# Triangular inverse of the RWKV-7 chunk scan: 32x32 diagonal blocks, off-diagonal block by two products

## The chip, the cores and the metric

One core of a Trainium2 chip runs the whole program. The metric is device time in microseconds (us) of one execution, the median of several runs. Engines: PE (TensorE matmul; PEld is its weight load), DVE (VectorE), ACT (ScalarE), POOL (GpSimd), SP (its queue issues most DMAs).

## The reference, cut to what matters

A first block (attention and a Mamba scan), then a second block of two layers on 512 tokens plus 256 context tokens. One half of layer 0 is an RWKV-7 mixer: 8 heads of 64 channels, run over the tokens in both directions.

```python
def rwkv7_scan(r, w, k, v, kk, b, s0):
    def step(s, inp):
        r_t, w_t, k_t, v_t, kk_t, b_t = inp
        sa = jnp.einsum('bhvk,bhk->bhv', s, kk_t)
        s = s * w_t[:, :, None, :] - sa[..., None] * b_t[:, :, None, :] + v_t[..., None] * k_t[:, :, None, :]
        return s, jnp.einsum('bhvk,bhk->bhv', s, r_t)
```

The kernel does not step token by token. It takes chunks of 64 tokens; inside a chunk the terms `sa` depend on each other through a triangular 64x64 matrix A per head, so the kernel needs the inverse of (I + A) for each head, direction and chunk.

## The kernel before, in words

The program is one long stream of weight units (512 KB of fp32 each) that SP loads into three buffers, ACT rounds (`whi`, L292), DVE takes the rest of (`wlo`, L293), and PE multiplies in three products (L301 to L303, L384 to L386). The scan of layer 0 runs inside that stream: `mix0_scan` (L1647) walks 12 steps, 4 on the context and 8 on the tokens, and between the pieces of a step it emits pieces of other work: the token projections and `rwkv_prep` first, then the context's output projection and FFN. The order on each engine is then set by a scheduler of the framework, which orders instructions by its own cost estimates before the program is built; on the chip each engine works its list in order.

A step treats one chunk per direction (d), 4 pairs of heads (b), and the two heads of a pair in the two halves of the partitions (e): 16 triangles of 64x64, held as a tile of 128 partitions x 512 columns (d, b, 64). Three generators make a step:

- `scores(i)` (L1504): loads AR, KB and v, multiplies them (L1513), masks (L1516, `Sc`), copies the triangle part into A (L1521, POOL for e = 0 and ACT for e = 1), then writes AR over the copied part of Sc (L1523).
- `inverse(i)` (L1543): level 0 on DVE (L1554, L1555, and L1557, a transpose into Tm), then five levels l = 1 to 5, each of which doubles the size of the inverted blocks: POOL masks the level's part out of A (`Al`, L1550); 16 matmuls Tm, Al (L1563); ACT copies the result out of PSUM into W (L1565); 16 matmuls with X and W (L1573); DVE subtracts (L1576) and transposes (L1577), or on the last level subtracts into X6 (L1581).
- `serial(i)` (L1584): F (L1603), U = X6 times f (L1609), the new state (L1616 to L1622), the output (L1629, L1632).

While step i is in `serial(i)` and then `scores(i+2)`, `inverse(i+1)` runs beside it (`tail`, L1676). These matmuls are fp32, and each appears as two rows of PE and two of PEld: 16 matmuls make 32 rows. They use a part of the array: `tile_position` gives its first row and column, so that the two heads of a pair sit in different quarters of the array.

```python
for d, b in DB:
    for e, h in enumerate(H):
        mm(ps[h, d, b], Al[h, d, b], Tm[h, d, b], start=True, stop=True, tile_position=(64 * e, 64 * e))
```

For comparison the text also uses L1030 (`ada_units`): fp32 matmuls of 128 rows into 32 columns with 256 moving columns, on four column strips of the array in turn, and L1041, fp32 matmuls with 128x128 weights and 32 moving columns.

## Time and profile before

| | |
|---|---|
| median of 3 runs | 3386.49 us (3383.27 to 3392.45) |
| the profiled execution | 3376.74 us |
| its span, first to last instruction | 3375.0 us |
| PE busy | 3163.2 us, 94% |
| DVE busy | 2023.6 us, 60% |
| ACT busy | 1378.6 us, 41% |
| POOL busy | 238.0 us, 7% |
| the scan | about 1390 to 2160 us of the span |

A row of a group of instructions reads: line, engine, operation, tile written <- tiles read, shape, count | busy us, mean ns of one | idle us of the engine just before them and what ended it. A row of a stretch gives start:end, its length, the busy us of PE, PEld, DVE, ACT and POOL with the number of instructions that ran in it, the granted clock of PE (1.00 is full), and the DMA share and rate. A matmul's own duration contains its way through the array; matmuls that follow each other overlap, so the distance between starts is what a matmul costs.

### The profile page before, as it was taken

What the parts mean: (1) busy time and instruction counts of PE and PEld (TensorE: products, weight loads), DVE (VectorE), ACT (ScalarE), POOL (GpSimd) and SP (SyncE); (2) the same over time, 40 slices, a digit from 0 to 9 for tenths busy, and PEclk for the clock granted to TensorE, in tenths of its full rate; (3) what the DMA queues carried; (4) which work ended last, traced back from release to release, by engine and by line L of the source; (5) the groups of instructions that cost most, each with busy time, mean ns of one, the idle gap of its engine ahead of it and who ended that gap; (6) DMA issues with size and microseconds to landing.
All of it is one profiled execution on the core that took longest, in us unless ns stands there. A gap on an engine that the chain in (4) does not pass through costs nothing.

```text
span 3375.0 us, 51306 instructions
## 1 busy us (share of the span) xinstructions
PE 3163.2 (94%) x20798; PEld 2539.0 (75%) x20798; DVE 2023.6 (60%) x3274; ACT 1378.6 (41%) x2301; POOL 238.0 (7%) x276
## 2 busy tenths in 40 slices
PE   8999999998899999888898999989999989899998
PEld 7777777776777788666677888768788767778886
DVE  3344576775556533557665666667475754776756
ACT  3344334332354432434344444456432444543323
POOL 0000000000100000121121122000000210000001
PEclk9999999999999999899899999999999999999999
DMA  6222344435434432444545554633322425232333
GB/s 205 81 70 70 120 156 137 134 123 190 163 114 131 131 111 94 134 125 118 159 162 173 163 170 148 203 136 99 106 94 94 137 91 184 72 113 89 99 99 108
DMA packets 216493, 430.85 MB, mean 128 GB/s; under 512 B 75114, under 2 KB 114218, under 8 KB 216000
## 3 DMA queue, kind: packets, MB, share of 16 engines
q1 hardware_dynamic: 192896, 367.83, 34.5%
q10 hardware_dynamic: 20912, 51.64, 4.1%
q0 software_dynamic: 2448, 8.09, 0.8%
q8 instruction: 164, 2.69, 0.3%
q14 instruction: 73, 0.60, 0.1%
HBM read 380.70 MB, written 46.79 MB: 127 GB/s over the span
## 4 chain that ended last, share of the span: by engine, by line
PE 76%; DVE 10%; DMA 6%; ACT 4%; issue 3%; POOL 1%; SPq 0%; ACTq 0%; POOLq 0%; DVEq 0%
PE psa L301 11%; PE psa L303 11%; PE psa L302 11%; PE psa L384 6%; PE psa L385 6%; PE psa L386 6%; PE pso L301 3%; PE pso L302 3%; PE pso L303 3%; DVE wlo L293 3%; PE psa L1563 1%; ACT whi L292 1%; PE psa L1573 1%; PE pso L1030 1%; PE pso L384 1%
## 5 line engine op out<-in xcount | busy, mean ns | idle before, releaser
L293 DVE TENSOR_TENSOR wlo<-wraw,whi 128x1024 fp32r<-128x1024 f32 x480 | 597.2, 1245 | 483.6 <-ACT whi L292 482.6
L292 ACT CAST whi<-wraw 128x1024 fp32r<-128x1024 f32 x482 | 503.7, 1046 | 740.1 <-PE psa L386 258.8
L301 PE MATMUL psa<-xh,wlo 128*128 128x512 f32 (+1 forms) x1760 | 693.4, 396 | 15.6 <-DVE wlo L293 12.1
L303 PE MATMUL psa<-xh,whi 128*128 128x512 f32 (+1 forms) x1760 | 685.0, 390 | 0.0
L302 PE MATMUL psa<-xl,whi 128*128 128x512 f32 (+1 forms) x1760 | 684.0, 390 | 0.0
L301 PEld LDWEIGHTS psa<-xh,wlo 128*128 128x128 f32 x1760 | 335.7, 192 | 95.0 <-DVE wlo L293 15.5
L303 PEld LDWEIGHTS psa<-xh,whi 128*128 128x128 f32 x1760 | 336.0, 191 | 72.5 <-issue 5.1
L302 PEld LDWEIGHTS psa<-xl,whi 128*128 128x128 f32 x1760 | 336.6, 192 | 70.6 <-issue 3.9
L1151 DVE SCALAR_TENSOR_TENSOR fc<-psa,f_cv,fc 128x441 f32<-128x441 f32 (+2 forms) x352 | 243.5, 693 | 41.4 <-ACT fc L1140 34.6
L301 PE MATMUL pso<-xh,wlo 128*128 128x256 f32 (+1 forms) x720 | 231.2, 321 | 0.0
L302 PE MATMUL pso<-xl,whi 128*128 128x256 f32 (+1 forms) x720 | 221.5, 308 | 1.0 <-DVE xl L347 1.0
L303 PE MATMUL pso<-xh,whi 128*128 128x256 f32 (+1 forms) x720 | 220.6, 306 | 0.0
L385 PE MATMUL psa<-wlo,ah 128*128 128x512 f32 x528 | 211.1, 400 | 2.8 <-DVE wlo L293 2.5
L384 PE MATMUL psa<-whi,al 128*128 128x512 f32 x528 | 209.2, 399 | 3.4 <-ACT whi L292 3.4
L386 PE MATMUL psa<-whi,ah 128*128 128x512 f32 x528 | 210.0, 398 | 0.0
L301 PEld LDWEIGHTS pso<-xh,wlo 128*128 128x128 f32 x720 | 136.4, 189 | 11.9 <-issue 1.7
L302 PEld LDWEIGHTS pso<-xl,whi 128*128 128x128 f32 x720 | 136.4, 189 | 9.8 <-issue 1.7
L303 PEld LDWEIGHTS pso<-xh,whi 128*128 128x128 f32 x720 | 136.2, 189 | 7.5 <-issue 0.4
L385 PEld LDWEIGHTS psa<-wlo,ah 128*128 128x128 f32 x528 | 99.2, 188 | 29.9 <-DVE wlo L293 6.3
L384 PEld LDWEIGHTS psa<-whi,al 128*128 128x128 f32 x528 | 99.0, 188 | 29.5 <-ACT whi L292 4.7
L384 PE MATMUL psa<-whi,xl 128*128 128x512 f32 x288 | 116.9, 408 | 4.4 <-DVE h L941 2.7
L385 PE MATMUL psa<-wlo,xh 128*128 128x512 f32 x288 | 116.8, 406 | 0.0
(559 smaller groups left out, 5119.1 us busy)
## 6 DMA issues: line engine op xcount, KB each, us to landing
wraw<-in_f_up_dram SPq DMA_DIRECT2D x132, 512.0 KB
wraw<-in_ada_w_dram SPq DMA_DIRECT2D x96, 512.0 KB
wraw<-in_f_dn_dram SPq DMA_DIRECT2D x66, 512.0 KB
wraw<-in_w_fi_dram SPq DMA_DIRECT2D x44, 512.0 KB
wraw<-in_ab_f_dram SPq DMA_DIRECT2D x38, 512.0 KB
wraw<-in_w_qk_dram SPq DMA_DIRECT2D x24, 512.0 KB
wraw<-in_w_xbc_dram SPq DMA_DIRECT2D x24, 512.0 KB
wraw<-in_c_f_dram SPq DMA_DIRECT2D x24, 512.0 KB
```

The costliest lines, as they stand in the source:

```text
L292: nc.scalar.copy(hi, raw)
L293: (eng or nc.vector).tensor_tensor(lo, raw, hi.bitcast(F32), op=ALU.subtract)
L301: mm(ps, wl, xh, start=start, stop=False)
L302: mm(ps, wh, xl, start=False, stop=False)
L303: mm(ps, wh, xh, start=False, stop=stop)
L384: mm(ps, sl, wh[:, c], start=first and k == 0, stop=False)
L385: mm(ps, sh, wl[:, c], start=False, stop=False)
L386: mm(ps, sh, wh[:, c], start=False, stop=last and k == kbn - 1)
L1030: nc.tensor.matmul(ps[o:o + 32], self.cs[:, 4 * h + j, 22 - 2 * i:54 - 2 * i], raw[:, j * 256:(j + 1) * 256], start=h == 0, stop=h == 1, t ...
L1151: V_.scalar_tensor_tensor(o, pv[:, r0 + dr:r1 + dr, c0 + dc:c1 + dc], cw(i), o, op0=ALU.mult, op1=ALU.add)
L1563: mm(ps[h, d, b], Al[h, d, b], Tm[h, d, b], start=True, stop=True, tile_position=(64 * e, 64 * e))
L1573: mm(ps[h, d, b], lt[h, d, b], rt[h, d, b], start=True, stop=True, tile_position=(64 * e, 64 * e))
```

## The change

The 64x64 triangle is cut into two 32x32 diagonal blocks and one 32x32 off-diagonal block. `A` holds the diagonal blocks of all four 32-partition strips in 256 columns, `Ao` the off-diagonal block in 128 columns (four copies of 32 partitions each on POOL and on ACT in place of one copy of 64 each). `inverse` runs levels 0 to 4 on the diagonal blocks, in tiles of 256 columns, with 32 matmuls of 32x32 on the four diagonal 32x32 tiles of the array in the place of 16 of 64x64. The last level becomes two products of 16 matmuls of 32x32 (`Ao` with `Tm`, then `Wo` with `X`). X6 is now one tile, set to zero once; the diagonal blocks are copied into it and the second product is written into it negated. The mask table shrinks from 1600 to 1120 columns.

```diff
-    for b in (1, 2, 4, 8, 16, 32):
-        lev.append(f2(((s // b) % 2 == 0) & (t // b == s // b + 1)))
-        lev.append(f2(((s // b) % 2 == 1) & (t // b == s // b - 1)))
-    lev.append(f2(s == t))
+    s, t = p % 32, np.arange(32)[None, :]
+    for b in (1, 2, 4, 8, 16):
+        lev.append(((s // b) % 2 == 0) & (t // b == s // b + 1))
+        lev.append(((s // b) % 2 == 1) & (t // b == s // b - 1))
+    lev.append(s == t)
...
+        Q = [[slice(64 * e + 32 * r, 64 * e + 32 * r + 32) for r in range(2)] for e in range(2)]
+        C = [slice(0, 32), slice(32, 64)]
+        X6 = pool.tile([P, 2, 4, 64], F32, name="X6", bufs=1)
+        G_.memset(X6, 0.0)
...
-            A = BA[i] = first.tile([P, 2, 4, 64], F32, name="A", bufs=1)
+            A = first.tile([P, 2, 4, 32], F32, name="A", bufs=1)
+            Ao = first.tile([P, 4, 32], F32, name="Ao", bufs=1)
+            BA[i] = A, Ao
             for e in range(2):
-                (G_.tensor_copy, S_.copy)[e](A[H[e]], Sc[H[e], :, e, :, 0])
+                for r in range(2):
+                    (G_.tensor_copy, S_.copy)[e](A[Q[e][r]], Sc[Q[e][r], :, e, :, 0, C[r]])
+                    (G_.tensor_copy, S_.copy)[e](Ao[Q[e][r]], Sc[Q[e][r], r, e, :, 0, C[1 - r]])
...
+            def prod(ps, lt, rt):
+                for d, b in DB:
+                    for q in range(4):
+                        h = slice(32 * q, 32 * q + 32)
+                        mm(ps[h, d, b], lt[h, d, b], rt[h, d, b], start=True, stop=True, tile_position=(32 * q, 32 * q))
...
-            for l in range(1, 6):
-                ps = v8(self.ptile())
-                for d, b in DB:
-                    for e, h in enumerate(H):
-                        mm(ps[h, d, b], Al[h, d, b], Tm[h, d, b], start=True, stop=True, tile_position=(64 * e, 64 * e))
-                W = new("W", 1)
+            for l in range(1, 5):
+                ps = w4(self.ptile())
+                prod(ps, Al, Tm)
+                W = part4("W", 1)
                 S_.copy(W, ps)
-                if l < 5:
+                if l < 4:
                     Al = part(l + 1)
                 yield
-                ps = v8(self.ptile())
-                for d, b in DB:
-                    for e, h in enumerate(H):
-                        lt, rt = (X, W) if l < 5 else (W, X)
-                        mm(ps[h, d, b], lt[h, d, b], rt[h, d, b], start=True, stop=True, tile_position=(64 * e, 64 * e))
-                if l < 5:
-                    Tn, Xn = new("Tm"), new("X")
-                    V_.tensor_tensor(Tn, Tm, ps, op=ALU.subtract)
-                    V_.transpose(fl(Xn), fl(Tn))
-                    Tm, X = Tn, Xn
-                else:
-                    XI[i] = new("X6", 1)
-                    V_.tensor_tensor(XI[i], X, ps, op=ALU.subtract)
-                yield
+                ps = w4(self.ptile())
+                prod(ps, X, W)
+                Tn, Xn = part4("Tm"), part4("X")
+                V_.tensor_tensor(Tn, Tm, ps, op=ALU.subtract)
+                V_.transpose(fl(Xn), fl(Tn))
+                Tm, X = Tn, Xn
+                yield
+            ps = self.ptile()[:, :128].rearrange("p (b v) -> p b v", b=4)
+            for b in range(4):
+                for e in range(2):
+                    for d in range(2):
+                        k, o = Q[e][d], Q[e][1 - d]
+                        mm(ps[o, b], Ao[k, b], Tm[k, d, b], start=True, stop=True, tile_position=(k.start, o.start))
+            W = pool.tile([P, 4, 32], F32, name="Wo", bufs=1)
+            S_.copy(W, ps)
+            for e in range(2):
+                for r in range(2):
+                    (G_.tensor_copy, S_.copy)[e](X6[Q[e][r], :, :, C[r]], X[Q[e][r]])
+            yield
+            ps = self.ptile()[:, :128].rearrange("p (b v) -> p b v", b=4)
+            for b in range(4):
+                for e in range(2):
+                    for d in range(2):
+                        k, o = Q[e][d], Q[e][1 - d]
+                        mm(ps[k, b], W[o, b], X[o, d, b], start=True, stop=True, tile_position=(o.start, k.start))
+            for e in range(2):
+                for d in range(2):
+                    dst, src = X6[Q[e][d], d, :, C[1 - d]], ps[Q[e][d]]
+                    if e:
+                        S_.activation(dst, src, AF.Copy, scale=-1.0)
+                    else:
+                        V_.tensor_scalar(dst, src, -1.0, None, op0=ALU.mult)
+            XI[i] = X6
+            yield
```

How the lists of the engines change is shown at three places. The first is PE in the last step but one, where U (X6 times f) is followed by the first products of the next inverse. Before:

```order
L386 MATMUL pso<-whi,ah 128x512
L1609 MATMUL psb<-f,X_18116 64x64 x16
L1563 MATMUL psa<-Tm,Al 64x64 x16
L301 MATMUL pso<-xh,wlo 128x256
L302 MATMUL pso<-xl,whi 128x256
```

And now (the line numbers are those of the changed file: L303 to L305 are the old L301 to L303, L1571 is the matmul in `prod`):

```order
L388 MATMUL pso<-whi,ah 128x512
L1648 MATMUL psb<-f,X_10640 64x64 x16
L1571 MATMUL psa<-Tm,Al 32x32 x32
L303 MATMUL pso<-xh,wlo 128x256
L304 MATMUL pso<-xl,whi 128x256
```

The burst stands at the same place between the same neighbours; 16 matmuls of 64x64 have become 32 of 32x32.

The second place is PE in the middle of the scan, at the end of an inverse. Before, the last burst of the last level:

```order
L303 MATMUL pso<-xh,whi 128x256
L1030 MATMUL pso<-wraw,cs 32x256 x8
L1539 MATMUL psb<-masks,KB_16369 128x128 x4
L1573 MATMUL psa<-X,W 64x64 x16
L301 MATMUL pso<-xh,wlo 128x256
```

Now, with L1612 the second product of the off-diagonal block:

```order
L305 MATMUL pso<-xh,whi 128x256
L1032 MATMUL pso<-wraw,cs 32x256 x8
L1550 MATMUL psb<-masks,KB_17538 128x128 x4
L1612 MATMUL psa<-X,Wo 32x32 x16
L303 MATMUL pso<-xh,wlo 128x256
```

Here 16 matmuls stay 16, of a quarter of the size, again at the same place.

The third place is ACT at the end of the same inverse. Before (L1521 and L1523 belong to the scores of the step after next, L292 to the weight units, L1140 and L1156 to the context's FFN):

```order
L1523 COPY Sc<-AR_16361 64x4x64
L1523 COPY Sc<-AR_16367 64x4x64
L1521 COPY A<-Sc 64x512
L1565 COPY W<-psa 128x512
L292 CAST whi<-wraw 128x1024
L1533 COPY vs<-psb 64x2x2x64 x2
L1140 ACTIVATE fc<-pso,f_cb,f_cv 128x256
L1540 COPY Ns<-psb 128x4x2x64
```

Now:

```order
L1531 COPY A<-Sc 32x256 x2
L1583 COPY W<-psa 128x256
L294 CAST whi<-wraw 128x1024
L1544 COPY vs<-psb 64x2x2x64 x2
L1605 COPY X_10640<-X 32x8x32 x2
L1142 ACTIVATE fc<-pso,f_cb,f_cv 128x256
L1551 COPY Ns<-psb 128x4x2x64
L1532 COPY Ao<-Sc 32x128
L1534 COPY Sc<-AR_17530 64x4x64
L1534 COPY Sc<-AR_17536 64x4x64
L1532 COPY Ao<-Sc 32x128
L1158 ACTIVATE fc<-fc 128x256
L1602 COPY Wo<-psa 128x128
```

The two copies of AR into Sc have moved from ahead of the A copy to the end of the inverse. They stand between the two copies of Ao, and Ao has one buffer, which the first off-diagonal product (L1600) of the running inverse still reads.

## Rows read from the trace of the kernel before

**Rows 1.** The page: PE's busy row, and the chain of waits by engine.
```profile
PE 3163.2 (94%) x20798; PEld 2539.0 (75%) x20798; DVE 2023.6 (60%) x3274; ACT 1378.6 (41%) x2301; POOL 238.0 (7%) x276
PE 76%; DVE 10%; DMA 6%; ACT 4%; issue 3%; POOL 1%; SPq 0%; ACTq 0%; POOLq 0%; DVEq 0%
```

**Rows 2.** Stretches of the scan: length, busy PE, PEld, DVE, ACT, POOL, clock.
```profile
1390.00:1700.00 310.00, 258.59 (x2702) 191.61 (x2700) 203.52 (x289) 138.03 (x255) 63.52 (x68) 0.87 0.45 132
1700.00:1850.00 150.00, 134.77 (x1911) 110.70 (x1908) 94.70 (x155) 61.98 (x117) 29.80 (x32) 0.95 0.51 168
1850.00:2160.00 310.00, 302.04 (x4149) 265.36 (x4149) 200.77 (x301) 146.65 (x230) 51.27 (x51) 1.00 0.50 159
```

**Rows 3.** Groups by line, 1390 to 2160 us: bursts of the inverse, and L1513.
```profile
L1563 PE MATMUL psa<-Tm,Al 64*64 64x64 f32 x1920 | 76.0, 230 | 16.7 <-DVE Tm L1576 11.8 <-POOL vs L1502 2.3 <-POOL Al L1550 1.3
L1573 PE MATMUL psa<-W,X 64*64 64x64 f32 x1536 | 57.7, 223 | 0.2 <-ACT W L1565 0.2
L1513 PE MATMUL psa<-AR,KB 64*128 64x128 f32 x384 | 32.5, 304 | 10.5 <-DMA AR<-za 5.4 <-DMA KB<-zk 5.1
```

**Rows 4.** Timeline of PE, three places: start us, us, line, rows in the burst.
```profile
1433.67 1.07 PE L1030 MATMUL pso<-wraw,cs 128*32 128x256 f32 x16
...
1447.10 1.15 PE L1563 MATMUL psa<-Tm,Al 64*64 64x64 f32 x32
...
1896.40 1.16 PE L1513 MATMUL psa<-AR,KB 64*128 64x128 f32 x16
1897.49 1.15 PE L1573 MATMUL psa<-W,X 64*64 64x64 f32 x32
```

**Rows 5.** Two short stretches at a burst's start: L1030, then L1563.
```profile
1433.66:1433.70 0.04, 0.03 (x4) 0.03 (x5) 1.00 0.00 0
...
1447.09:1447.14 0.05, 0.04 (x2) 0.04 (x2) 1.00 0.00 0
```

**Rows 6.** Stretches of 0.03 and 0.02 us at the start of one L1041 group.
```profile
660.68:660.71 0.03, 0.01 (x1) 0.01 (x1) 1.00 0.00 0
660.71:660.73 0.02, 0.02 (x2) 0.02 (x1) 1.00 0.50 205
```

**Rows 7.** Bursts of L1563 by stretch of the scan: busy us and count.
```profile
1390.00:1700.00 310.00, 26.65 (x640) 23.67 (x640) 0.87 0.45 132
1700.00:1850.00 150.00, 19.70 (x448) 16.94 (x448) 0.95 0.51 168
1850.00:2160.00 310.00, 29.69 (x832) 26.64 (x832) 1.00 0.50 159
```

**Rows 8.** Waits of PE from 1390 to 1850 us: us in total, times, longest.
```profile
PE pso L1415 <- DVE kds L1413: 11.2, 4, 4.1
PE psa L1563 <- DVE Tm L1576: 9.6, 5, 3.8
PE psa L1513 <- DMA AR<-za: 5.4, 2, 4.2
```

**Rows 9.** Waits of PE from 1850 to 2160 us.
```profile
PE psa L1563 <- POOL vs L1502: 2.3, 1, 2.3
PE psa L1563 <- DVE Tm L1576: 2.2, 4, 0.9
```

**Rows 10.** Groups by line, 1390 to 2160 us: the other engines.
```profile
L1565 ACT COPY W<-psa 128x512 f32<-128x512 f32 x60 | 35.1, 585 | 61.1 <-PE psa L1563 57.2 <-issue 2.9 <-ACT yo L1638 0.9
L1577 DVE STREAM_TRANSPOSE X<-Tm 128x512 f32<-128x512 f32 x48 | 33.9, 706 | 0.8
L1576 DVE TENSOR_TENSOR Tm<-Tm,psa 128x512 f32<-128x512 f32 x48 | 32.6, 680 | 18.3 <-PE psa L1573 18.3
L1550 POOL TENSOR_TENSOR Al<-A,masks 128x512 f32<-128x512 f32 x60 | 85.9, 1433 | 410.4 <-PE psa L1563 394.2 <-DVE xn L332 15.7
L1604 DVE COPY f<-psb 128x256 f32<-128x256 f32 x12 | 5.0, 418 | 6.0 <-PE psb L1603 5.9
L1604 ACT COPY f<-psb 128x256 f32<-128x256 f32 x12 | 4.5, 373 | 2.9 <-PE psb L1603 2.9
```

More of the change, by code (lines that the diff above doesn't have):

```diff
@@ L1543, in inverse @@
         def inverse(i):
-            A = BA.pop(i)
-            lev = lambda l: self.mlev[:, l].unsqueeze(2).to_broadcast([P, 2, 4, 64])
+            A, Ao = BA.pop(i)
+            lev = lambda l: self.mlev[:, l].unsqueeze(2).to_broadcast([P, 2, 4, 32])
+            part4 = lambda n, k=2: pool.tile([P, 2, 4, 32], F32, name=n, bufs=k)
+            w4 = lambda ps: ps[:, :256].rearrange("p (d b v) -> p d b v", d=2, b=4)
             def part(l):
-                r = new("Al")
+                r = part4("Al")
@@ L1550, in part @@
                 G_.tensor_tensor(r, A, lev(l), op=ALU.mult)
                 return r
+            def prod(ps, lt, rt):
[3 more added lines that the diff above has]
+                        mm(ps[h, d, b], lt[h, d, b], rt[h, d, b], start=True, stop=True, tile_position=(32 * q, 32 * q))
             Al = part(1)
-            X = new("X")
+            X = part4("X")
             V_.tensor_tensor(X, A, lev(0), op=ALU.mult)
-            V_.tensor_tensor(q8(X), self.id2.unsqueeze(1).to_broadcast([P, 8, 64]), q8(X), op=ALU.subtract)
@@ L1556, in inverse @@
-            Tm = new("Tm")
+            V_.tensor_tensor(q8(X), self.id2.unsqueeze(1).to_broadcast([P, 8, 32]), q8(X), op=ALU.subtract)
+            Tm = part4("Tm")
             V_.transpose(fl(Tm), fl(X))
             yield
-            for l in range(1, 6):
-                ps = v8(self.ptile())
-                for d, b in DB:
-                    for e, h in enumerate(H):
-                        mm(ps[h, d, b], Al[h, d, b], Tm[h, d, b], start=True, stop=True, tile_position=(64 * e, 64 * e))
-                W = new("W", 1)
+            for l in range(1, 5):
+                ps = w4(self.ptile())
+                prod(ps, Al, Tm)
+                W = part4("W", 1)
@@ L1608, in serial @@
                 for e, h in enumerate(H):
-                    mm(U[h, d, b], X6[h, d, b], f[h, d, b], start=True, stop=True, tile_position=(64 * e, 64 * e))
+                    mm(U[h, d, b], X6_[h, d, b], f[h, d, b], start=True, stop=True, tile_position=(64 * e, 64 * e))
             S_.activation(vu[H[0], :, 0], U[H[0]], AF.Copy, scale=-1.0)
```

10 lines of the change are left out of this document (5 added, 5 removed).

## The prediction

> **What bounds the kernel now.** I read the page first: PE is busy 94% of the span and holds 76% of the chain of waits [rows 1]. The change touches the scan only, so the next view is the scan in three stretches [rows 2]. They differ. From 1390 to 1700 us, where the context's and the tokens' inputs are still being prepared, PE is busy 258.6 of 310 us and its clock is 0.87 of full: there PE waits for others. From 1700 to 1850 us it is busy 134.8 of 150 us. From 1850 to 2160 us it is busy 302 of 310 us at full clock, with DVE at 201, ACT at 147 and POOL at 51 us: there PE alone sets the pace. The waits of PE say the same. Up to 1850 us the largest are for DVE's preparation of the inputs (11.2 us in four waits), for the subtraction of the inverse (9.6 us in five) and for a load (5.4 us) [rows 8]; after 1850 us the two largest are 2.3 and 2.2 us [rows 9]. The inverse's share: of the 1920 rows of L1563 in all, 640 lie in the first stretch, 448 in the second and 832 in the third [rows 7], so of the 12 inverses 4, 2.8 and 5.2. The scheduler's lists place every burst of the changed kernel between the same neighbours, so what a burst loses or gains PE meets at the same spot.
>
> **What a burst costs.** An inverse is ten bursts of 32 rows, each 1.15 us from first start to last end [rows 4]; a row alone lasts 0.22 to 0.23 us [rows 3]. That leaves 0.93 us from first to last start. Two rows start together, one per quarter of the array in use (two within 0.05 us [rows 5]), so the burst is 16 pairs, 0.93 / 15 = 0.062 us apart. The burst of L1513 has 16 rows with weights of 128 columns and 128 moving columns, also two by two; its rows last 0.30 us in the mean [rows 3], as little as 0.27 us by the same share as above, and the whole 1.16 us [rows 4], so 8 pairs are (1.16 - 0.27) / 7 = 0.127 us apart. Double the columns, double the distance: 0.065 us for 64 columns. Half of 64 columns should then take 0.062 - 0.032 = 0.030 us.
>
> **How many rows run side by side.** The new products use four separate tiles of the array in turn. The trace has no 32x32 tile. The nearest row is L1030, four column strips in turn: four of its rows start within 0.04 us [rows 5], and its 16 rows of 256 moving columns, 0.385 us each, are over in 1.07 us [rows 4], which only fits four at a time. Issuing is therefore fast enough for four rows in 0.04 us at a burst's start. Whether it holds over 64 rows is not shown: the fastest whole burst has 0.93 us for 32 rows, 0.029 us a row [rows 4]. These are the bounds for the price of a row: 0.030 / 4 = 0.0075 us (four side by side) and 0.029 us (no faster than seen over a whole burst). I take the lower end, since L1030 shows four tiles at once and the distance between rows has followed the columns so far; L1041 has two rows with 32 moving columns that both start within 0.05 us [rows 6], so a row so short need not hold the array for the 0.062 us of a 64-column pair.
>
> **The sum on PE.** A burst of 32 matmuls is 64 rows, 16 groups of four: 15 x 0.030 + 0.04 for the spread of four starts + 0.22 for the last row = 0.71, with a slightly longer first gap 0.73 us. A burst of 16 (the two off-diagonal products) is 8 groups: 7 x 0.030 + 0.04 + 0.22 = 0.47 us. One inverse: before 10 x 1.15 = 11.5 us, now 8 x 0.73 + 2 x 0.47 = 6.8 us, a gain of 4.7 us. The number of bursts stays ten, so what lies at a burst's edge is paid as often as before. Where the clock is at half a row saves twice as much; I leave that out.
>
> **What of it reaches the end.** Third stretch: 5.2 x 4.7 = 24.4 us, PE is the bound, I keep 95% (23). Second: 2.8 x 4.7 = 13.2 us, a tenth of the time PE waits; I keep 80% (10.5). First: 18.8 us, a sixth of the time PE waits, mostly on DVE's preparation, which does not get shorter with PE's burst; I keep half (9.4). Together 43 us.
>
> **The other engines.** DVE's work per inverse halves in columns: a subtraction of 512 columns takes 0.68 and a transpose 0.71 us; the row nearest to the new subtraction is the copy of 256 columns out of PSUM with 0.42 us [rows 10]. Four levels save about 4 x (0.27 + 0.33) = 2.4 us, level 0 and the last level about 1.2 us more. DVE is at 65% in the third stretch and waited for little, so I count nothing; if DVE were the bound, as in parts of the first stretch, it would add up to 3.6 us an inverse. POOL's mask of a level falls from 1.43 us towards half, one level goes, and six small copies come in place of one, none with more columns than a half mask; POOL is busy 51 of 310 us. The memset of X6 and the smaller mask table are done once, long before. ACT is the engine that gets more: five copies of W of 0.585 us become four of 0.373 us (the ACT row of L1604) and one shorter, but A, Ao and X6 add seven small copies of 0.2 to 0.4 us [rows 10]: +0.7 us an inverse, at 147 of 310 us hidden.
>
> **The new wait.** Ao has one buffer. Its copies for the step after next must wait for the first off-diagonal product (L1600) of the running inverse, and the copies of AR into Sc must wait for them. On ACT what stands behind them is Wo, which needs the same product anyway, and then a weight copy (L294), on which PE's weight units depend. From the end of that product ACT needs two Ao copies, two copies of 256 columns (0.37 us, the same row) and one activation before Wo, about 2 us, while PE has some 25 rows of the context's FFN and a weight-unit burst, about 4 us, before it needs Wo. So it is covered by the three weight buffers and that work; if the cover fails, ACT stalls 1 to 4 us in each of ten steps. I take off 3 us, so 40 us are left. The profiled execution took 3376.7 us; 40 us less is 3336.7 us. It lies 9.8 us below the median of the runs shown, 3386.5 us, so on the footing of the median the forecast is **3347 us**.
>
> **Rivals.**
> 1. *Rows cannot be issued so fast.* Price per row 0.029 us, the upper bound: a burst of 64 rows takes 64 x 0.029 + 0.2 = 2.05 us, one of 32 rows stays at 1.15. An inverse then costs 8 x 2.05 + 2 x 1.15 = 18.7 us, 7.2 us more, 86 us over twelve; with the same shares as above (5.2, 2.8, 4 inverses at 95, 80, 50%) 66 us, so about 3452 us. It decides from 0.0165 us a row on: there 576 rows and ten ends of 0.2 us make the old 11.5 us. Against it speak the four rows in 0.04 us; for it, that no burst of the trace keeps that up. The Trainium skill has a rule for this (TensorE: Matmul & The Clock Gate, "Wait — 56ns, not 53.3ns?"): matmuls start no closer than about 25 ns however few columns they have. By that figure a burst would be an estimated 1.8 us and the kernel some 45 us slower, near 3432 us; the trace disagrees for rows on different tiles, of which two and four start well within that time [rows 5]. Chance 0.12.
> 2. *A group of four takes as long as a pair does now, or only two run side by side.* Then a burst of 64 rows is 16 x 0.062 + 0.2, the same 1.15 us, and only the two small bursts gain, 2 x 0.48 = 1 us an inverse: 9 us realised, less the 3 us for ACT, 3380 us. The Trainium skill speaks for this one (TensorEngine Tiling (Array Packing), "Instruction Overhead"): a matmul with few moving columns lasts as long as one with 60, and no tiling factor should be taken from a dimension that is already small. By it a group of four would be an estimated 0.06 us. The two rows of L1041 [rows 6] speak against it. Chance 0.10.
> 3. *PE gets shorter but something else takes its place*: weights that come late because ACT stands before the Ao copies, or DVE's preparation. A third to a half of the 43 us would be left, 3366 to 3372 us. For it: PE's waits in the first two stretches [rows 8]. Against: the third stretch waits for nearly nothing. Chance 0.12.
>
> **How the numbers follow.** A measurement of this kernel tells about 0.3%, 10 us, from no change. The forecast has 0.66: 3347 us, from 3325 (all 57 us of PE, and a little of DVE's and the chain's) to 3362. Rival 3 is still faster by more than 0.3% in most of its cases, rival 2 in about half of its cases no longer. Faster: 0.66 + 0.10 + 0.02 = 0.78; the same: 0.02 + 0.08 = 0.10; slower: 0.12. The range runs from 3322 to 3382 us, which takes in rivals 2 and 3 and leaves out rival 1 and a few hundredths below.
>
> **What would show it.** Bursts of 64 rows at 0.7 to 0.75 us and small ones near 0.47 us in the timeline of PE; PE's busy time of the inverse lines down by about 55 us; the scan's end some 40 us earlier, and nothing changed after it. Rival 1 shows as bursts of 1.8 to 2.1 us, rival 2 as bursts still at 1.15 us, rival 3 as short bursts with new waits of PE for ACT's `whi` or DVE. The forecast is wrong in its price if the burst is not within 0.65 to 0.85 us, and in its shares if the burst is right and the scan is not 30 to 55 us shorter.

## The result and the profile after

The change takes **3353.24 us** (median of 4 runs, 3348.93 to 3358.08), the kernel before, run beside it on the same chip, 3387.31 us (3383.27 to 3392.45). The ratio is 0.990 with a 95% interval of 0.9885 to 0.9915: 1% faster, 34 us. The forecast was 3347 us with a range of 3322 to 3382. The profiled execution of the change took 3358.08 us with a span of 3356.3 us; it lies 4.8 us above its median, that of before 9.8 us below its own, so the two traces are only 18.7 us apart. Rows are compared with that in mind.

The busy row of the page of the change, against [rows 1]:

```profile
PE 3133.9 (93%) x23870; PEld 2503.7 (75%) x23870; DVE 1979.6 (59%) x3286; ACT 1389.8 (41%) x2385; POOL 225.5 (7%) x325
```

PE works 29 us less. The same three stretches of the scan as in [rows 2] (length, busy PE, PEld, DVE, ACT, POOL, granted clock, DMA share and rate):

```profile
1390.00:1700.00 310.00, 253.05 (x3852) 182.54 (x3853) 193.87 (x306) 145.41 (x292) 62.58 (x89) 0.85 0.43 133
1700.00:1850.00 150.00, 130.64 (x2623) 107.65 (x2621) 86.21 (x156) 64.96 (x133) 22.26 (x38) 0.93 0.54 178
1850.00:2160.00 310.00, 291.53 (x5545) 248.11 (x5544) 191.44 (x323) 152.13 (x271) 46.90 (x73) 0.98 0.53 178
```

The instructions on PE went up in every stretch while its busy time went down, and its clock lies 0.02 lower in each. The stretches are cut at the same times, so the last one now holds 21 us of what follows the scan. DVE has less to do everywhere, ACT a little more. The groups of the inverse from 1390 to 2160 us (line, shapes, count | busy us, mean ns | idle before), against [rows 3]; L1571 is the product of a level, L1600 and L1612 the two off-diagonal products:

```profile
L1571 PE MATMUL psa<-Tm,Al 32*32 32x32 f32 x3072 | 40.6, 198 | 10.7 <-DVE Tm L1590 8.5 <-issue 2.2
L1571 PE MATMUL psa<-W,X 32*32 32x32 f32 x3072 | 39.9, 199 | 3.9 <-issue 2.6 <-ACT W L1583 1.0
L1600 PE MATMUL psa<-Tm,Ao 32*32 32x32 f32 x384 | 5.6, 197 | 0.2 <-DVE Tm L1590 0.2
L1612 PE MATMUL psa<-X,Wo 32*32 32x32 f32 x384 | 5.5, 194 | 1.7 <-ACT Wo L1602 1.7
```

Together they are busy 91.6 us. Before, the two groups of [rows 3] were busy 133.7 us, and the rest of L1573, its last level, stands here:

```profile
L1573 PE MATMUL psa<-X,W 64*64 64x64 f32 x384 | 14.6, 229 | 1.8 <-ACT W L1565 1.8
```

That makes 148.3 us, so the inverse lost 56.7 us of PE. Single bursts in the timeline of PE (start us, us, line, rows in the burst), against [rows 4]:

```profile
1898.99 0.75 PE L1571 MATMUL psa<-W,X 32*32 32x32 f32 x64
...
1904.26 0.45 PE L1600 MATMUL psa<-Tm,Ao 32*32 32x32 f32 x32
1906.54 0.45 PE L1612 MATMUL psa<-X,Wo 32*32 32x32 f32 x32 [0.31 <-ACT Wo L1602]
```

64 rows in 0.75 us: after a last row of 0.19 us, (0.75 - 0.19) / 63 = 0.009 us a row. The starts in the trace show two paces in this burst. The first 32 rows start in fours, four rows within 0.020 us and, after a first gap of 0.053 us, 0.032 us from one four to the next. From about the 40th row on they start in twos, 0.0167 us from one two to the next.

**Where the time came from.** One burst per step, U (L1609 before, L1648 now), makes a mark that the change did not touch. The marks of the fourth, sixth, seventh and twelfth step, and the first matmul of what follows the scan, before the change:

```profile
1702.76 1.15 PE L1609 MATMUL psb<-f,X 64*64 64x64 f32 x32
...
1807.27 0.92 PE L1609 MATMUL psb<-f,X 64*64 64x64 f32 x24 [0.38 <-DVE X L1581]
...
1879.39 1.15 PE L1609 MATMUL psb<-f,X 64*64 64x64 f32 x32
2154.92 1.15 PE L1609 MATMUL psb<-f,X 64*64 64x64 f32 x32
2162.91 0.92 PE L1732 MATMUL psb<-masks,Yn 64*64 64x64 f32 x24
```

and after it:

```profile
1695.02 1.15 PE L1648 MATMUL psb<-f,X 64*64 64x64 f32 x32
...
1794.72 0.29 PE L1648 MATMUL psb<-f,X 64*64 64x64 f32 x2 [0.58 <-DVE X L1619]
...
1869.78 1.15 PE L1648 MATMUL psb<-f,X 64*64 64x64 f32 x32
2130.92 1.15 PE L1648 MATMUL psb<-f,X 64*64 64x64 f32 x32
2138.91 0.91 PE L1771 MATMUL psb<-masks,Yn 64*64 64x64 f32 x24
```

The scan begins at the same place within 1 us. By step 4 the change is 7.7 us ahead, by step 6 12.6 us, by step 7 only 9.6 us, by step 12 24.0 us. So the stretches up to step 4, to step 7 and to the end gave 7.7, 1.9 and 14.4 us, and in the middle one step gave 3.0 us back. From the end of the scan to the end of the span both take about the same (3375.0 - 2162.9 = 1212.1 us and 3356.3 - 2138.9 = 1217.4 us; two other profiles below, of the change repeated and of the kernel before with a small edit, have 1221.5 and 1218.2 us). In a second profile of the change, of the repeat below, the marks of steps 4, 7 and 12 lie at 1691.38, 1866.44 and 2124.64 us, which is 11.4, 1.6 and 17.3 us. The middle stretch gave next to nothing in both.

**Where the rest of the 57 us stayed.** The whole scan, from its first scores matmul to the first matmul behind it, before and after (columns as in the stretches):

```profile
1392.91:2162.91 770.00, 695.40 (x8805) 567.61 (x8805) 500.36 (x749) 345.73 (x600) 144.59 (x151) 0.94 0.48 150
```

```profile
1392.01:2138.91 746.90, 656.04 (x11877) 525.33 (x11877) 456.44 (x761) 356.13 (x684) 131.73 (x200) 0.92 0.48 155
```

The scan is 23 us shorter. PE's idle time in it rose by 16 us (74.6 to 90.9), and its busy time fell by only 39 us although the inverse's own rows lost 57: the other rows of PE took some 17 us longer. That goes with the clock, at whose lower level a row takes nearly twice as long: in the change the same eight rows of L340 take 1.97 us at 1815.66 us, where the granted clock is 0.50, and 1.09 us at 1823.51 us, where it is 1.00. So in this pair of profiles about half of what did not arrive is new idle time and half is slower rows. The pair overstates the second half, since over all runs the mean granted clock is 0.968 for the kernel before (34 runs) and 0.966 for the change (8 runs), against 0.972 and 0.963 in these two profiles. In the profiles of the repeat and of the kernel before with a small edit, both below, the two parts are 13 and 10 us.

The idle time by what ended it, before and after: DVE 41 and 48 us, ACT 18 and 22, DMA 11 and 14, POOL 5 and 0, no engine 0 and 6. How it splits between DVE and ACT differs from profile to profile (47 and 46, 9 and 21 us in the second pair); the two together rose by 11 us in the first pair and by 12 in the second. The waits of PE in the change, 1385 to 2265 us (us in total, times, longest), against [rows 8, 9]:

```profile
PE pso L1417 <- DVE kds L1415: 17.9, 4, 10.6
PE psa L1519 <- DMA AR<-za: 8.9, 4, 7.0
PE psa L1571 <- DVE Tm L1590: 8.5, 11, 2.5
...
PE psa L1571 <- issue: 4.8, 6, 1.4
```

The rows left out here have one that is nearly new: PE's wait for DVE's `vu` (L1655), 7.8 us in three waits, the longest 6.0 us in the first stretch; before, it was 0.4 us. The longest wait of all, 10.6 us for kds, is in the first stretch too. Two windows of the change, around the wait for kds and the longest wait for AR:

```profile
1636.00:1648.00 12.00, 1.37 (x4) 0.73 (x4) 11.09 (x16) 5.36 (x10) 3.73 (x4) 0.50 0.45 113
...
1805.00:1815.00 10.00, 2.90 (x38) 2.36 (x35) 2.47 (x6) 4.58 (x10) 1.13 (x2) 0.84 0.86 322
```

In the first, PE works 1.37 of 12 us (columns as above), and DVE 11.09 of 12 us, nearly all of it on the preparation of the tokens' inputs; the wait on kds was at most 4.1 us before [rows 8] and is 10.6 us now. The same product before the change:

```profile
1651.64 2.08 PE L1415 MATMUL pso<-kds,masks 128*128 128x512 f32 x2 [3.83 <-DVE kds L1413]
```

Now it starts at 1647.26 us. So PE asked for it 11 us sooner and DVE had it ready 4.4 us sooner. The 10.6 us are not all new: before, PE also waited 2.1 us for ACT and 3.8 us for `Tm` in the 13 us ahead of this product, and one wait has taken the place of three. In the second, PE works 2.9 of 10 us and the DMAs move 322 GB/s. There it waits for AR, the scores' input of a step:

```profile
1814.09 1.65 PE L1519 MATMUL psa<-AR,KB 64*128 64x128 f32 x10 [7.00 <-DMA AR<-za]
```

SP's queue shows why. Its rows in the change, and then the same load before the change:

```profile
1792.55 7.58 SPq L293 DMA_DIRECT2D wraw<-in_f_up_dram  x2
...
1805.37 0.80 SPq L1498 DMA_DIRECT2D AR<-za  x2
```

```profile
1818.82 0.80 SPq L1492 DMA_DIRECT2D AR<-za  x2
...
1825.20 1.65 PE L1513 MATMUL psa<-AR,KB 64*128 64x128 f32 x12 [4.22 <-DMA AR<-za]
```

SP issues the load of AR when PE has read the buffer for the last time: it waits 2.9 us for that (L1671), and waited 5.0 us for it before. So the load is issued 13.5 us earlier, but PE can go on only 8.7 us after that (1814.09 - 1805.37), where it was 6.4 us before. The DMAs, asked for two weight units just ahead, are busy for 0.86 of the window, and were for 0.94 of the same place before (1816 to 1826 us). From the first of these two issues to PE's going on it is 20.4 us before (1825.20 - 1804.79) and 21.5 now: a time that did not shrink with PE's bursts. The wait cost 2.8 us more than before, in the step that gave 3.0 us back. What the bursts of that step gained went at two waits for DVE, 1.7 us for `fc` at 1852.36 us and 1.3 us for `wlo` at 1861.07 us. A third place is the inverse itself in the last stretch: after 1850 us its wait for `Tm` went from 2.2 us in four waits [rows 9] to 5.3 us in five. One of these waits in the timeline, two rows of DVE and one of PE:

```profile
1943.68 1.23 DVE L295 TENSOR_TENSOR wlo<-wraw,whi 128x1024 fp32r<-128x1024 f32 x1 [1.40 <-ACT whi L294]
...
1945.42 0.41 DVE L1590 TENSOR_TENSOR Tm<-Tm,psa 128x256 f32<-128x256 f32 x1
...
1945.98 0.27 PE L1571 MATMUL psa<-Tm,Al 32*32 32x32 f32 x3 [2.55 <-DVE Tm L1590]
```

The subtraction is short now (0.41 us), but it stands behind a weight unit's `wlo` in DVE's order, and PE is back 2.55 us before it.

### The profile page after: what moved, and what is told of

The parts are those of the page before. It is cut to its first block, busy times and chain, and to the rows that moved or that the text cites. A ratio compares the mean times of both kernels' runs of the same rounds, so it can differ in the third digit from the quotient of the medians.

```text
span 3356.3 us, 57588 instructions
## 1 busy us (share of the span) xinstructions
PE 3133.9 (93%) x23870; PEld 2503.7 (75%) x23870; DVE 1979.6 (59%) x3286; ACT 1389.8 (41%) x2385; POOL 225.5 (7%) x325
## 4 chain that ended last, share of the span: by engine, by line
PE 76%; DVE 9%; DMA 7%; ACT 4%; issue 3%; POOL 1%; SPq 0%; ACTq 0%; POOLq 0%; DVEq 0%
PE psa L303 12%; PE psa L305 11%; PE psa L304 11%; PE psa L386 6%; PE psa L387 6%; PE psa L388 6%; PE pso L303 3%; PE pso L304 3%; PE pso L305 3%; DVE wlo L295 2%; DMA wraw<-in_f_up_dram 1%; PE pso L1032 1%; ACT whi L294 1%; PE psa L1571 1%; PE pso L780 1%
## 5 line engine op out<-in xcount | busy, mean ns | idle before, releaser
L303 PE MATMUL psa<-xh,wlo 128*128 128x512 f32 (+1 forms) x1760 | 696.0, 397 | 14.3 <-DVE wlo L295 10.6
L305 PE MATMUL psa<-xh,whi 128*128 128x512 f32 (+1 forms) x1760 | 687.2, 391 | 0.0
L303 PEld LDWEIGHTS psa<-xh,wlo 128*128 128x128 f32 x1760 | 338.0, 193 | 94.1 <-DVE wlo L295 14.6
L305 PEld LDWEIGHTS psa<-xh,whi 128*128 128x128 f32 x1760 | 337.4, 192 | 73.5 <-issue 5.1
L303 PE MATMUL pso<-xh,wlo 128*128 128x256 f32 (+1 forms) x720 | 233.0, 324 | 2.0 <-DVE wlo L295 1.3
L305 PE MATMUL pso<-xh,whi 128*128 128x256 f32 (+1 forms) x720 | 221.8, 308 | 0.0
L303 PEld LDWEIGHTS pso<-xh,wlo 128*128 128x128 f32 x720 | 137.2, 191 | 12.6 <-issue 2.8
L305 PEld LDWEIGHTS pso<-xh,whi 128*128 128x128 f32 x720 | 137.3, 191 | 8.5 <-issue 1.4
L388 PEld LDWEIGHTS psa<-whi,ah 128*128 128x128 f32 x528 | 99.5, 188 | 23.5
```

The lines of the kernel that those rows point to most:

```text
L303: mm(ps, wl, xh, start=start, stop=False)
L305: mm(ps, wh, xh, start=False, stop=stop)
L388: mm(ps, sh, wh[:, c], start=False, stop=last and k == kbn - 1)
```

## The experiments

The theory to test: the gain is PE's shorter bursts, four tiles side by side, of which a part is lost again at places where PE waits for something that the change did not shorten. Its rivals: the gain does not come from the width (two tiles would do), it comes from elsewhere (fewer columns on DVE and ACT), or the missing part is lost to the change's own new steps (the wait for Ao, ACT's small copies, the off-diagonal products).

Twelve kernels ran, in three sets on three chips, each set beside the kernel before (medians 3384.42, 3393.08 and 3389.91 us). Across sets only the ratios to before are compared; 0.001 of ratio is 3.4 us. The change stands at 0.990 in the first comparison and 0.9898 in the repeat; "above the change" below means against 0.9899.

### The change once more

> The change itself once more, beside the three variants on the same chip. Every theory: its ratio to the kernel before again between 0.987 and 0.993, so about 3353 us (3346 to 3360).

Measured: 3355.54 us (3350.21 to 3361.93), ratio 0.9898 (0.9871 to 0.9925). The gain holds in a second set.

### Two tiles at a time instead of four

```diff
-                for d, b in DB:
-                    for q in range(4):
+                for q2 in (0, 2):
+                    for d, b in DB:
+                        for q in (q2, q2 + 1):
...
```

> Only the order of the 32 matmuls in a burst changes: first the two upper tiles in turn, then the two lower ones, so that two rows instead of four can run side by side; ACT, DVE, POOL and the place of every burst stay as in the changed kernel. Theory 1 (the gain is the shorter bursts of PE, and they are short because four tiles run side by side): 32 pairs about 0.031 us apart, a burst of 64 rows 1.2 to 1.25 us instead of 0.75, PE +0.48 us in each of 96 bursts = +46 us, of which 60 to 80% reach the end: 3381 to 3390 us, about where the kernel before stands. Theory 2 (the gain comes from the halved tiles of DVE, ACT and POOL and the shorter chain of an inverse): within 10 us of 3353.

Measured: 3372.05 us, ratio 0.9958 (0.9941 to 0.9975), 20 us above the change (14 to 26).

Its timeline of PE:

```profile
1904.38 1.11 PE L1572 MATMUL psa<-W,X 32*32 32x32 f32 x64
```

The burst grew by 1.107 - 0.753 = 0.354 us in the median, 34 us over 96 bursts, of which 20 us, 59%, came through. The burst grew less than theory 1 had it (1.2 to 1.25 us), so the time lies just below its range; it lies above theory 2's. Two wide, the kernel is still 14 us faster than the kernel before. The off-diagonal products account for 9 us of that (below), and the levels' bursts are 0.04 us shorter than the 1.15 us of before. No run separates what is left from the halved tiles of DVE and ACT.

### One tile at a time

```diff
-                for d, b in DB:
-                    for q in range(4):
+                for q in range(4):
+                    for d, b in DB:
...
```

> Again only the order within a burst: all eight matmuls of one tile, then of the next, so that nothing runs side by side. Theory 1: if rows on one tile are paced as the groups are now, 64 x 0.031 + 0.22 = 2.2 us a burst, PE +1.45 us x 96 = +139 us, 60 to 90% of it at the end: 3436 to 3478 us. If a tile's weight load cannot lie beside its own matmul, a row takes about 0.06 us, a burst 4 us, +312 us of PE: 3540 us and more. Theory 2: within 20 us of 3353. The run prices side-by-side work by itself.

Measured: 3446.71 us, ratio 1.0180 (1.0153 to 1.0208), 95 us above the change. Its timeline of PE:

```profile
1929.45 1.91 PE L1571 MATMUL psa<-W,X 32*32 32x32 f32 x64
```

The same 64 rows take 0.75 us four tiles wide, 1.11 us two wide, 1.91 us one wide. The order in which the tiles are named decides whether rows run side by side: one tile at a time would have made the change slower than the kernel before. The time lies in theory 1's range; its burst, 2.2 us, was too long. The added PE time is (1.91 - 0.75) x 96 = 111 us, and 86% of it came through. The more PE time is added, the larger the share that counts: at the margin around the change 59%, over 111 us 86%.

### Two buffers for the off-diagonal block

```diff
-            Ao = first.tile([P, 4, 32], F32, name="Ao", bufs=1)
+            Ao = first.tile([P, 4, 32], F32, name="Ao", bufs=2)
```

> Ao gets a second buffer, so its copies for the step after next no longer wait for the running inverse's first off-diagonal product, and AR is copied into Sc early again. Theory 1 (that wait is covered): within 5 us of 3353. Rival (ACT stands in front of the Ao copies and the weights behind it come late, which is where 20 us of PE's saving went): 8 to 20 us faster, 3333 to 3345.

Measured: 3352.82 us, ratio 0.9898 (0.9876 to 0.9920), the change's own. The waits of the Ao copies for PE in the change, POOL's and ACT's (us, times, longest):

```profile
POOL Ao L1532 <- PE psa L1600: 17.2, 7, 7.4
...
ACT Ao L1532 <- PE psa L1600: 2.1, 2, 1.4
```

With two buffers both waits for the first off-diagonal product are gone from the trace (both engines wait for DVE's `Sc` there), and nothing was won by it: it was covered.

### Each level's product twice

```diff
-                for d, b in DB:
-                    for q in range(4):
...
+                for _ in range(2):
+                    for d, b in DB:
+                        for q in range(4):
...
```

> Each product of the four levels is computed twice into the same place, so a burst has 128 rows; the result and the other engines' work are unchanged. Theory 1: +16 groups x 0.0317 = +0.51 us a burst, 1.26 us, +49 us of PE; the same 60 to 80% at the end as was gained: 3382 to 3392 us. If all of it reaches the end (the gain was cut by something else than waits of PE): 3402. Theory 2: within 10 us of 3353.

Measured: 3465.96 us (3451.95 to 3469.25), ratio 1.0225 (1.0194 to 1.0256), 110 us above the change, where no theory had more than 50. The burst itself is about as short as it should be (1.29 us for 128 rows, forecast 1.26), but 45 times a burst stops in the middle or before it begins:

```profile
1906.96 0.55 PE L1572 MATMUL psa<-W,X 32*32 32x32 f32 x41
1908.33 0.94 PE L1572 MATMUL psa<-W,X 32*32 32x32 f32 x87 [0.81 <-issue]
...
1927.73 1.29 PE L1572 MATMUL psa<-Tm,Al 32*32 32x32 f32 x128
```

The waits of PE name no engine for it (us, times, longest):

```profile
PE psa L1572 <- issue: 52.5, 45, 3.0
...
PE psb L1669 <- issue: 4.2, 3, 3.7
PE psa L1519 <- issue: 3.7, 2, 3.2
```

The added PE time is (1.29 - 0.75) x 96 = 51 us, and these three rows alone are 60 us, where such waits were 6 us in the change. Together that is about the 110 us, if all of it reaches the end; in the two orders above 59 and 86% did, so the sum alone proves nothing. The DMA queue that carries instructions has an own row on the page (packets, MB, share). In the change, and then with the products doubled:

```profile
q8 instruction: 187, 3.06, 0.4%
```

```profile
q8 instruction: 235, 3.85, 0.5%
```

The doubled products add 6144 matmuls and as many weight loads, 12288 instructions, and 48 packets: 256 instructions and about 16 KB each. The theory for the next runs: PE's instructions come in blocks of 256, and dense short rows use up a block faster than the next arrives. The traces bear out the blocks: with PE's instructions counted in order, all 51 waits of more than 0.25 us that no engine ends (1385 to 2300 us) fall at the same place of a block of 256, and so do the 42 and 29 such waits of the next two runs and the 7 of the change. The kernel before has none.

### The second product over 4 columns

```diff
-                for d, b in DB:
-                    for q in range(4):
-                        mm(ps[h, d, b], lt[h, d, b], rt[h, d, b], ...)
+                for n in (32, 4):
+                    for d, b in DB:
+                        for q in range(4):
+                            mm(ps[h, d, b, :n], lt[h, d, b], rt[h, d, b, :n], ...)
```

> Each level's product is followed by a second one over 4 of its 32 columns, so a burst has as many instructions as with the product done twice (128 rows) but the second half streams an eighth of the columns. The four 4-column columns that it writes again hold the same values. Theory A (the excess over the sum when the product was done twice is PE's instruction supply: idle time inside bursts at every 256th instruction, 65.8 us there): that idle time stays, 40 us or more in all, and the time stays far above the change, 3420 to 3470 us. Theory B (the excess came from the work in the array, for example a lower granted clock or bank conflicts of the doubled columns): hardly any idle time inside the bursts, and the time within 20 us of the change, 3353 to 3375.

Measured: 3480.37 us, ratio 1.0268 (1.0233 to 1.0304), 125 us above the change and 10 us above theory A's range. Its timeline of PE, a whole burst and the second part of one that stops after 48 rows:

```profile
1911.58 1.26 PE L1572 MATMUL psa<-W,X 32*32 32x32 f32 x128
...
1920.10 0.85 PE L1572 MATMUL psa<-W,X 32*32 32x32 f32 x80 [0.87 <-issue]
```

and among its waits of PE:

```profile
PE psa L1572 <- issue: 49.2, 36, 4.9
PE psb L1669 <- issue: 5.6, 2, 3.4
PE pso L304 <- issue: 2.9, 3, 1.6
```

The stops stayed with an eighth of the columns in the second half: they come with the number of instructions, not with the columns that move through the array, as theory A said. The bursts hardly became shorter either (1.26 us against 1.29, with a last row of 0.17 against 0.19 us), so a row costs (1.26 - 0.17) / 127 = 0.0086 us, against (1.29 - 0.19) / 127 = 0.0087: in the second half of such a burst a row of 4 columns costs what a row of 32 does. The weight loads are the same in both runs, so whether the issue of instructions or the weight loads set that pace is not shown. Bursts (+0.50 x 96 = 48 us) and stops (57.7 us in these rows, some 6 us in the change) make 100 of the 125 us. The granted clock from 1390 to 2290 us was 0.87 here against 0.92 in the change and 0.91 with the products doubled; that fits the rest, but no run separates it.

### Doubled, and two tiles at a time

```diff
+                for _ in range(2):
+                    for q2 in (0, 2):
+                        for d, b in DB:
+                            for q in (q2, q2 + 1):
...
```

> Each level's product twice (128 rows), in the order that keeps two tiles in work at a time, so that the same number of instructions is taken at half the rate, 16 ns apiece instead of 8. PE time: two bursts of 1.1 us for one of 0.75, +1.4 us x 96 = +130 us. Theory A1 (PE's instruction supply falls behind because of the rate of the rows): the idle time that the waits put down to issue falls from 52.5 us to under 20 us, although the number of instructions is the same. Theory A2 (each block of instructions costs a fixed stop, whatever the rate): it stays at 45 to 60 us. One look, no verdict on the time; 3430 to 3500 us.

Measured, one run: 3495.67 us. The row of its waits that answers to L1572 above:

```profile
PE psa L1573 <- issue: 25.2, 32, 2.4
```

With the same number of instructions at 0.015 us a row (1.11 us for 64) instead of 0.0086, the stops on this row fell from 52.5 to 25.2 us: by half, neither under 20 us nor unchanged. They depend on the pace, but they do not vanish at half of it. It is one run, and its own price was not taken apart.

### The last level on 64x64 again

Levels 1 to 4 stay, the last level goes back to 64x64 products.

```diff
-            ps = self.ptile()[:, :128].rearrange("p (b v) -> p b v", b=4)
-            for b in range(4):
-                for e in range(2):
-                    for d in range(2):
-                        k, o = Q[e][d], Q[e][1 - d]
-                        mm(ps[o, b], Ao[k, b], Tm[k, d, b], start=True, stop=True, tile_position=(k.start, o.start))
+            ps = v8(self.ptile())
+            for d, b in DB:
+                for e, h in enumerate(H):
+                    mm(ps[h, d, b], Ao[h, d, b], TD[h, d, b], start=True, stop=True, tile_position=(64 * e, 64 * e))
...
+            X6 = new("X6", 1)
+            V_.tensor_tensor(X6, XD, ps, op=ALU.subtract)
```

The diagonal blocks of X and Tm are copied into full-width tiles first (`XD`, `TD`), so ACT, POOL and DVE have more to do here too. It ran in two forms. In the first, `Ao` is a single tile that the copies of a later step write before this step's product reads it, so that product works on another step's block (the same amount of work, and no wait):

> Levels one to four stay on 32x32 tiles; the last level is done as before, by 64x64 products with block-diagonal operands and a subtraction of the full width. Its two bursts should go from 0.45 us back to 1.15, so +1.4 us per inverse or +17 us of PE time over 12. Theory 1 (a saving on PE reaches the end at the 55 to 85 per cent that the two orders in the burst showed): +9 to +14 us, 3362 to 3367 us. Theory 2 (the off-diagonal block's own steps, the extra wait on the narrow eviction and the four small copies into X6, cost what its short bursts save): within 4 us of the change, 3349 to 3357.

Measured: 3360.23 us, ratio 0.9910 (0.9885 to 0.9936), 4 us above the change. In the second, each step has its own block:

> The last level by 64x64 products once more, here with two buffers for the off-diagonal block that alternate by step, so that one step's copies never reach another step's product and no copy waits for it. As before this edit, +17 us of PE time (two bursts of 1.15 us for two of 0.45, 12 times). Theory 1 (a PE saving reaches the end at 55 to 85 per cent): 3362 to 3367 us. Theory 2 (the off-diagonal block's own small steps give its short bursts' saving back): within 4 us of the change.

Measured: 3365.90 us, ratio 0.9925 (0.9907 to 0.9943), 9 us above the change (3 to 15). Its bursts are the old ones in the timeline, here the first of the two:

```profile
1912.47 1.15 PE L1603 MATMUL psa<-TD,Ao 64*64 64x64 f32 x32
```

Of 12 x 1.4 = 17 us of PE, 9 us came through by the second form, 53%, at the lower edge of theory 1; the first form's interval also allows nothing. So the off-diagonal products carry about a quarter of the change's 34 us (3 to 15 us by the interval, the additional copies of this run included), and the four levels the rest.

### The small copies all on POOL

```diff
-                    (G_.tensor_copy, S_.copy)[e](A[Q[e][r]], Sc[Q[e][r], :, e, :, 0, C[r]])
+                    G_.tensor_copy(A[Q[e][r]], Sc[Q[e][r], :, e, :, 0, C[r]])
```

and likewise for Ao and X6.

> The four copies into A and Ao and the four copies into X6 all go to POOL, so that ACT loses six short copies per inverse (about 1.4 us of ACT) and POOL gains them. Theory 1 (the part of PE's saving that did not reach the end was lost to waits on the chain between stages and to DVE's kds work, not to ACT): within 5 us of the change, 3348 to 3358. Theory 2 (ACT, which gained small copies by the change, holds the level chain up): 5 to 15 us less, 3338 to 3348. Theory 3 (POOL's slower copies stand in the chain now): 5 us or more above the change.

Measured: 3361.06 us (3349.56 to 3370.40), ratio 0.9912 (0.9879 to 0.9945), 4 us above the change by the middle of the interval, 7 below to 16 above by its ends. Of theory 2's 5 to 15 us less the interval leaves only the first 2, so ACT's added copies are hardly what holds the change back; whether POOL's slower ones cost anything is inside the spread.

### The kds product one piece later

```diff
+            if T == SEQ:
+                yield "projected" if b == 3 else "wait"
             ps = self.fps()[:, :T]
             mm(ps, self.bd64, kds, start=True, stop=True)
...
```

The part of the diff that is left out lets the fourth piece count as the end of the projections. On the change:

> Filler units of 512 columns: the matmul on kds (line 1417) is issued one piece of the scan later than the multiplication that writes kds, and the fourth of them only after the projections count as finished. In the change PE waits 17.9 us there, 11.2 us before the change. Theory 1 (part of PE's saving of 54.6 us was lost because PE, early now, stands in order behind this matmul, while the scan's work is queued behind it): most of the wait goes, 8 to 17 us below the change, 3336 to 3345 us. Theory 2 (the wait only marks DVE's backlog, and the scan's products need DVE as well): the idle time comes back at the next products, at most 4 us below the change, 3349 or more.

and on the kernel before it:

> The same edit on the kernel before the change, with its 64x64 products. Theory 1: its wait of 11.2 us goes, 5 to 11 us below the kernel before, and the distance between this kernel and the change with the same edit is 37 to 44 us instead of 34, since the change had more to lose there. Theory 2: at most 4 us below the kernel before, and the distance stays at 30 to 37 us.

Measured: 3355.43 us (3339.96 to 3358.97), ratio 0.9887 (0.9867 to 0.9907), 4 us below the change by the middle of the interval; and 3386.66 us, ratio 0.9995 (0.9984 to 1.0005). Both times are theory 2's, but the edit did not do what it was made for. The same wait in the two kernels:

```profile
PE pso L1419 <- DVE kds L1415: 21.9, 4, 12.4
```

```profile
PE pso L1417 <- DVE kds L1413: 17.6, 4, 9.6
```

It became longer, in the kernel before too (17.9 and 11.2 us without the edit), though the product is one piece later in the list. The distance between the two kernels is 31 us, theory 2's 30 to 37. That agrees with DVE's backlog, which the window at 1636 us shows, but the price of the wait was not measured: the run that takes it away is missing. A third buffer for AR, which could let its load start ahead of the weight units at 1792 us, was not tried.

## Why the prediction was right, and where it was not

- **The burst.** Forecast 0.73 us for 64 rows, measured 0.75; forecast 0.47 us for 32, measured 0.45. PE's busy time of the inverse lines fell by 56.7 us, forecast 57. The step that mattered, taking 0.0075 us a row from four row starts in 0.04 us [rows 5] instead of the 0.029 us of the fastest whole burst [rows 4], held: 0.009 us. Its reason held for the first half of a burst, where the fours are 0.032 us apart (forecast 0.030). For the second half, twos 0.0167 us apart or 0.0083 us a row, the prediction had no row; that this other pace comes out so near is luck. Rival 1 would have been 2 us, and by the rule of the Trainium skill that the prediction weighed (TensorE: Matmul & The Clock Gate, "Wait — 56ns, not 53.3ns?") an estimated 1.8 us; the trace disagrees for rows that go to different tiles, and agrees on one tile, where a row costs (1.91 - 0.19) / 63 = 0.027 us in the mean of a burst.
- **Four tiles side by side.** Shown by the two orders: 0.75, 1.11 and 1.91 us. Two wide, the burst is as long as (1.11 - 0.19) / 31 = 0.030 us a pair makes it, the very distance that the prediction got by halving 0.062. Two wide, 64 rows take no longer than 32 rows of 64 columns did, just as rival 2 priced it; the rival failed because four run side by side.
- **The share that reached the end.** Forecast 43 us of 57, less 3; measured 34. By stretch, forecast 9.4, 10.5 and 23; measured 7.7, 1.9 and 14.4 in the first profile, 11.4, 1.6 and 17.3 in the second, each against one profile of the kernel before, so a few us of each are spread. By the prediction's own sign, a scan 30 to 55 us shorter, its shares fail in the first pair (24.0 us between the scans' ends) and just pass in the second (30.3). The step that failed most is the second stretch's "a tenth of the time PE waits; I keep 80%": a share read from the average of PE's idle time. Two steps there gained 4.9 us, and the third gave 3.0 back, at the load of AR, which is issued when PE is done with the buffer and then takes its time behind the weight units, and at two waits for DVE. The third stretch's 95% was too high as well: PE now meets DVE's order, with `wlo` ahead of the subtraction. No share of the prediction stands for PE's other rows getting slower, 10 to 17 us. Rival 3 ("something else takes its place") was at work in part. It named DVE and ACT, and PE's waits for the two together rose by 11 to 12 us; but ACT's wait at the Ao copies, which it named as a cause, cost nothing.
- **The lists.** The prediction took every burst to stand between the same neighbours in the changed kernel. By the two traces that holds for 70 of the 120 bursts, which start after the same number of other PE rows; of the 40 bursts of the first four inverses it holds for 14.
- **Marginal shares.** 59% (two tiles at a time; 41 to 76% by the run's interval), 53% (last level; 18 to 88%), 86% (one tile at a time): the share grows with the size of the step, though the small ones are loose. The change's own, 34 of 57 or 60%, sits with the small ones.
- **The Ao wait.** Forecast: covered, 3 us taken off for doubt. With two buffers the time is the same: covered (ACT waited 2.1 us in all), and the 3 us were not needed. They hid a third of the miss in the shares, which is luck.
- **ACT and DVE counted at nothing.** ACT's work grew by 11 us, 0.9 an inverse (forecast 0.7); that it costs nothing is borne out by the run with the copies on POOL, within its spread. DVE's work fell by 44 us, 3.7 an inverse (forecast 3.6), and no run shows what that brought. PE's longest wait for DVE, in the first stretch, is for the preparation, not for the inverse.
- **After the scan nothing changed**: 1212 and 1217 us, as forecast, within the spread of the four profiles (1212 to 1222 us).
- **Not foreseen:** stops on PE's instruction supply, 4.8 us at the products of the levels and 6 in all in the change.

## What to carry to other kernels

Small products gain from `tile_position` only if consecutive instructions go to different tiles, so check the order of the loops first: the same 64 rows took 0.75 or 1.91 us. When pricing what a shorter engine gives, don't scale by its average idle share: look in each stretch for the one transfer or engine that ends the longest wait, because there the saving mostly turns into a longer wait. Afterwards compare the engine's whole busy time with that of the changed rows: here 39 us against 57 showed that other rows had become slower. Count instructions as well as columns: in the doubled bursts 4 columns in place of 32 saved nothing, and the stops came at blocks of 256 instructions.

## What the runs showed of the hardware

- Rows on four 32x32 tiles follow one another every 0.0086 to 0.009 us over 64 to 128 rows. In the first 32 rows of a burst each tile takes a row every 0.032 us. That is also the distance of pairs on two tiles, and of most rows with one tile at a time. Later rows start in twos, 0.0167 us apart, and there 4 moving columns are no quicker than 32 (bursts of 128 rows 1.26 against 1.29 us). Whether issue or weight loads set that second pace is not shown.
- PE's instructions arrive in packets of 256 (48 packets for 12288 instructions), and dense rows outrun them: 60 us of stops with the products doubled, 25.2 us on the main row at half the pace, 4.8 us in the change. The Trainium skill (Runtime: NRT & Kernel Launch, "Instruction fetch mechanics") states the blocks of 256 and says that crossing one is mostly hidden; the trace agrees on the size and shows single stops of 3.0 us with the products doubled and 4.9 us with the narrow second product.
- PE's granted clock in the window 1636 to 1648 us, with PE busy 1.37 of 12 us, was 0.50, the lower of its two levels (1.2 of 2.4 GHz). It had fallen before that wait began: it was 0.51 from 1631 to 1636 us (PE busy 4.19 of 5 us), after 1.00 from 1620 to 1631 us (busy 9.90 of 11 us). Over the scan as a whole it was 0.92 (0.94 before the change), and PE's rows outside the inverse took 17 us longer in that pair of profiles.
